# A hybrid encoder layer: the delta half of the output projection by pairs of chunks in seven block products, k and q loaded for two scan steps at once, both directions' decays in one load

## The chip, the cores and the metric

The kernel runs on one core of a Trainium2 chip. Its engines work side by side, each through its own instructions in order: TensorE (PE) multiplies matrices into PSUM, and its weight loads stand in rows of their own (PEld); VectorE (DVE), ScalarE (ACT) and GpSimd (POOL) work on elements; SyncE (SP) issues all DMA transfers of this kernel. The metric is the device time of one execution in microseconds. The kernel before took 1280.27 us (median of 3 runs, 1278.16 to 1280.57).

## The reference

A layer on 2048 positions of width 1024: a normalised input is projected once; one group of heads runs a gated delta rule in both directions, another runs windowed attention; both results are concatenated, projected, and added to the input.

```python
h = rms_norm(x, norm_w[l])
proj = h @ w_in[l]
dn = gated_deltanet_bidir(dn_q, dn_k, dn_v, dn_beta, dn_decay, ...)   # forward + flipped backward
dn = rms_norm(dn, dn_out_norm_w[l]).reshape(b, s, DN_WIDTH) * silu(dn_z)
sw = windowed_gqa_with_sinks(sw_q, sw_k, sw_v, ...) * silu(sw_z)
mix = concatenate([dn, sw], axis=-1)
x = x + mix @ w_out[l]
```

In the delta rule each of 4 heads carries a 128 x 128 state through the sequence, chunk by chunk:

```python
v_new = u_i - w_i @ state
o = (q_i * exp(g_i)) @ state + a_i @ v_new
state = state * exp(g_last) + k_dec.T @ v_new
```

All is in float32. The big projections split each operand into a high part rounded to fp32r and a low rest, and add three products (high-high, low-high, high-low).

## The kernel before, in words

The sequence is cut into 16 chunks of 128. The first part (phase_a) projects, convolves, runs the attention, and leaves in DRAM: k and q of each head (kq_d), v (v_d), the gates (zdn, zsw_d) and the attention's output (mix_sw). delta_setup computes decays: gr_d holds the cumulated decay rows of each direction, and for head 0 the finished decay matrices go to DRAM as dec.

The second part (phase_b) goes through the 4 heads. For each head, pre_front loads k and q by four chunks (kq), v (vt) and the decays (gm, shown as dc in the profile), transposes, and forms the chunks' matrices (ma); heads 1 to 3 load a decay row broadcast over 128 partitions (line 664), add a mask on POOL (L665) and take the exponential on ACT. solve and invert invert the chunk matrices (tiles iv, b, g; products pi). scan then runs both directions side by side through 16 steps. In one step of a direction, with its line: pk (L812) is k times the state, r (L814, DVE), py (L821), yk and y (L826, L828, ACT), po (L823, L830, L839), the new state S (L833, DVE), and the sum of the output oacc (L846 to L850). From the second step on, each step loads its chunk's k and q (kqc, L810), 128 KB, into one of four buffers per direction.

After step 12, and again after the last, post normalises two groups of four chunks: eight squares with their sums (jko, L864, ACT), a power on POOL (sso, L868), scaling (L875, ACT), transposition (tro, L878), times the gate (zt, L881, DVE), and a store to mix_dn (L882). The second half of the output projection, for the attention's heads (sw_units, products pcs, L599 to L601, 32 units of 12 matmuls), fills PE between the scans of the heads; its sums go to DRAM as part.

After the last head's inversion the pools of that work are closed (L913), and the first four blocks of w_out are loaded and split (load_wo, tiles wos, woh, wol). out_dn then makes one chunk of the output, in the order of ORD, that is 7, 8, 6, 9 and so on from the middle outwards, as the two directions of the scan finish them: the mixed features (mxd) are loaded and split (mhd on ACT, mld on DVE), each half of 512 columns takes 4 x 3 matmuls (pcd, L561 to L563) into a PSUM bank, part is loaded (xrd) and added (L564), and the result is stored. Line numbers of the changed kernel differ: there scan's matmuls stand at 786, 795, 797, 804 and 813, pcs at 570 to 572, the output's at 959 to 961.

What order an engine works in is set at the end: set_order collects all instructions with their dependencies, gives each a cost in ns (such as `return max(112, 0.441 * m + 4)` for an fp32r matmul of m columns, and a flat 500 for issuing a DMA), plans forward and backward twelve times, and fixes the best order found on each of the five engines. The order in the code matters only through dependencies; a change at one place can move rows anywhere. In these dependencies two accesses of a tensor count as overlapping without regard to its first dimension, and in mix_dn that is the head.

Of the kernel before, what the change touches and what calls it, by code (L numbers as in the profile page):

```python
# [7 lines left out]
F32 = mybir.dt.float32  # L8
# [7 lines left out]
P = 128  # L16
# [8 lines left out]
NDEC = 1  # L25
SCRATCH = 1024
# [404 lines left out]
def delta_setup(tc, t, ident, bd, gp, ap, bp, pj, q_pool):  # L431
# [64 lines left out]
    gr_d = q_pool.tile([2, 64, P], F32, tag="gr_d", name="gr_d")  # L496
    for d in range(2):
        gt = pj.tile([P, 512], F32, tag="pj", name=f"gt{d}")[:64, :P]
        T.transpose(gt, gc[:, d], ident)
        gs = s1[:64, (5 + d) * P : (6 + d) * P]  # L500
        V.tensor_copy(gs, gt)
        dma(gr_d[d], gs)
    dec_d = {}
    for h in range(NDEC):
        for d in range(2):
            dec_d[h, d] = q_pool.tile([4, P, 512], F32, tag=f"dec{h}_{d}", name=f"dec{h}_{d}")
        for c4 in range(4):
            s4 = slice(4 * c4, 4 * c4 + 4)
            for d in range(2):
                gm = ap.tile([P, 4, P], F32, tag="gm", name=f"gm{h}_{c4}_{d}", bufs=2)  # L510
                src = gr_d[d].rearrange("(c h) i -> c h i", h=4)[s4, h]
                dma(gm, src.partition_broadcast(P))
# [3 lines left out]
                dma(dec_d[h, d][c4], gm.rearrange("p c i -> p (c i)"))  # L516
# [3 lines left out]
def phase_b(ctx, wide, late, tc, t, ident, consts, hp, mix_dn, mix_sw, kq_d, v_d, zdn_d, zsw_d, dp, out):  # L520
# [15 lines left out]

    def load_wo(pool, k0, name, tg=""):
        wh = pool.tile([P, 4, D], F32R, tag="woh" + tg, name=f"woh{name}", bufs=1)
        wl = pool.tile([P, 4, D], F32R, tag="wol" + tg, name=f"wol{name}", bufs=1)
        for k in range(4):  # L540
            for j in range(2):
                ns = slice(j * 512, (j + 1) * 512)
                sw = pool.tile([P, 512], F32, tag="ws", name=f"wos{name}_{k}_{j}")
                dma(sw, t["wout"][:, k0 + k, ns])
                A.activation(wh[:, k, ns], sw, AF.Copy)
                V.tensor_tensor(wl[:, k, ns], sw, wh[:, k, ns].bitcast(F32), ALU.subtract)
        return wh, wl

    def out_half(pool, bank, w, mx, src, dst, name, nb):
        wh, wl = w  # L550
        mh = pool.tile([P, 4, P], F32R, tag="mh", name=f"mh{name}", bufs=nb)
        ml = pool.tile([P, 4, P], F32R, tag="ml", name=f"ml{name}", bufs=nb)
        A.activation(mh, mx, AF.Copy)
        V.tensor_tensor(ml, mx, mh.bitcast(F32), ALU.subtract)
        for j in range(2):
            ns = slice(j * 512, (j + 1) * 512)
            xr = pool.tile([P, 512], F32, tag="ws", name=f"xr{name}_{j}")
            dma(xr, src[:, ns])
            ps = bank(j, f"pc{name}_{j}")
            for k in range(4):  # L560
                T.matmul(ps, mh[:, k], wh[:, k, ns], start=(k == 0), stop=False)  # L561
                T.matmul(ps, ml[:, k], wh[:, k, ns], start=False, stop=False)  # L562
                T.matmul(ps, mh[:, k], wl[:, k, ns], start=False, stop=(k == 3))  # L563
            V.tensor_tensor(xr, xr, ps, ALU.add)  # L564
            dma(dst[:, ns], xr)
# [51 lines left out]
    q1 = pool("q1", stack=pre_stack)  # L617
# [19 lines left out]
    def pre_front(h):  # L637
# [12 lines left out]
        for n, c4 in enumerate(FRONT):  # L650
# [6 lines left out]
            gms = []  # L657
            for d in range(2):
                gm = q1.tile([P, 4, P], F32, tag="gm", name=f"dc{h}_{c4}_{d}", bufs=4)
                if h < NDEC:  # L660
                    dma(gm.rearrange("p c i -> p (c i)"), dec_d[h, d][c4])
                else:
                    src = gr_d[d].rearrange("(c h) i -> c h i", h=4)[s4, h]
                    dma(gm, src.partition_broadcast(P))
                    G.tensor_tensor(gm, gm, dmask[:, d : d + 1].to_broadcast([P, 4, P]), ALU.add)  # L665
                gms.append(gm)
# [131 lines left out]
    def scan(h, H):  # L798
        ks, vs, ck, ma = (H[k] for k in ("ks", "vs", "ck", "ma"))
        oacc = H["oacc"] = {}  # L800
        st = {}
# [109 lines left out]
    for k in range(32):  # L911
        fill(1, bank(k % 2))
# [396 lines left out]
```

## Time and profile before

| | |
|---|---|
| median of 3 runs | 1280.27 us (1278.16 to 1280.57) |
| profiled execution | 1274.25 us, of it span 1272.5 us |
| granted clock of PE, mean | 0.992 |
| PE busy | 1219.4 us (96%) |
| DVE, ACT, POOL busy | 889.5, 703.2, 507.4 us |
| DMA packets | 225510, 205.34 MB |

In rows of single instructions or groups, the first number is the start or the total in us, then follow engine, line, operation, output <- inputs, shape, and after the bar the busy time, the mean ns of one, and the idle time of that engine just before, with what ended it. A row of a window gives its length, then for each engine busy us and instructions in brackets, then the granted clock of PE (1.00 is full), the share of the 16 DMA engines and GB/s. A row of loads gives count, size of one, and the median us from issue to landing. An fp32 matmul is recorded as two passes. Matmuls are pipelined: one of 512 columns is shown with some 390 ns, while the next one starts earlier.

### The profile page before, as it was taken

How to read it: one execution, taken by the hardware profiler on the slowest of the kernel's cores; microseconds unless marked ns; L12 is line 12 of the kernel's file. 1: busy time of each engine (PE TensorE's matmuls, PEld its weight loads, DVE VectorE, ACT ScalarE, POOL GpSimd, SP SyncE). 2: the span in 40 equal slices, each digit the busy share in tenths (PEclk: the TensorE clock that was granted, in tenths of full speed). 3: DMA queues.
4: the chain of work that ended last, by engine and by line, in shares of the span. 5: the costliest groups of instructions: out<-in, count | busy, mean ns of one | idle time of the engine just before them, and what ended most of it. 6: DMA issues, size and time to landing. Idle time of an engine off the chain costs nothing.

```text
span 1272.5 us, 22253 instructions
## 1 busy us (share of the span) xinstructions
PE 1219.4 (96%) x7066; PEld 1044.4 (82%) x7066; DVE 889.5 (70%) x2154; ACT 703.2 (55%) x2105; POOL 507.4 (40%) x893
## 2 busy tenths in 40 slices
PE   6999999999999999999999998998799899999998
PEld 6998877788889998787788787887688789798876
DVE  4422387999975589999986573788488879557333
ACT  6321254776644677776654425858557955566210
POOL 1330044666613398665221306613672651641000
PEclk9999999999999999999999998999899999999999
DMA  8442254322544434522137826967965974746675
GB/s 269 145 132 76 95 180 128 97 97 81 180 132 144 130 96 116 158 87 67 58 117 244 224 96 189 276 189 207 270 169 154 269 191 138 217 145 214 227 242 205
DMA packets 225510, 205.34 MB, mean 161 GB/s; under 512 B 48497, under 2 KB 175089, under 8 KB 225393
## 3 DMA queue, kind: packets, MB, share of 16 engines
q1 hardware_dynamic: 225392, 203.92, 52.7%
q8 instruction: 56, 0.92, 0.3%
q14 instruction: 62, 0.50, 0.1%
HBM read 138.79 MB, written 65.08 MB: 160 GB/s over the span
## 4 chain that ended last, share of the span: by engine, by line
PE 67%; DVE 12%; DMA 9%; ACT 7%; issue 3%; POOL 1%; SPq 0%; DVEq 0%; ACTq 0%; POOLq 0%
PE pf_c L191 4%; PE pf_c L192 4%; PE pf_c L193 4%; PE pf_z L191 4%; PE pf_z L192 4%; PE pf_z L193 4%; PE pi L772 4%; DVE acc L242 3%; PE pt L363 3%; PE pq_q L202 2%; PE pq_q L204 2%; PE pq_q L203 2%; PE pcd L561 2%; PE pcd L563 2%; PE pcd L562 2%
## 5 line engine op out<-in xcount | busy, mean ns | idle before, releaser
L191 PE MATMUL pf_c<-xhi,wh_c 128*128 128x512 f32 x384 | 151.0, 404 | 0.7 <-DVE acc L242 0.4
L192 PE MATMUL pf_c<-xlo,wh_c 128*128 128x512 f32 x384 | 150.6, 401 | 0.0
L193 PE MATMUL pf_c<-xhi,wl_c 128*128 128x512 f32 x384 | 149.1, 401 | 0.0
L242 DVE SCALAR_TENSOR_TENSOR acc<-pf_c,cw,acc 128x512 f32<-128x512 f32 (+1 forms) x192 | 140.3, 743 | 11.3 <-ACT acc L238 9.2
L358 POOL TENSOR_SCALAR pr<-pr,st 128x384 f32<-128x384 f32 (+1 forms) x128 | 80.1, 648 | 71.3 <-DVE st L356 60.0
L191 PE MATMUL pf_z<-xhi,wh_z 128*128 128x512 f32 x256 | 86.6, 401 | 0.5 <-DVE zo L215 0.5
L349 ACT ACTIVATE pr<-pr,st 128x384 f32<-128x384 f32 (+1 forms) x128 | 76.1, 596 | 19.6 <-DVE st L345 19.1
L192 PE MATMUL pf_z<-xlo,wh_z 128*128 128x512 f32 x256 | 86.2, 399 | 0.0
L191 PEld LDWEIGHTS pf_c<-xhi,wh_c 128*128 128x128 f32 x384 | 72.1, 188 | 15.3 <-DVE acc L242 1.7
L193 PE MATMUL pf_z<-xhi,wl_z 128*128 128x512 f32 x256 | 84.7, 397 | 0.0
L192 PEld LDWEIGHTS pf_c<-xlo,wh_c 128*128 128x128 f32 x384 | 72.3, 188 | 13.0
L193 PEld LDWEIGHTS pf_c<-xhi,wl_c 128*128 128x128 f32 x384 | 71.8, 188 | 13.0
L345 DVE CUSTOM_DVE_ANT_0 pr<-s,mask,sink 128x384 f32<-128x384 f32 (+1 forms) x128 | 72.5, 593 | 12.4 <-PE s L344 8.3
L367 ACT ACTIVATE ph<-pt 128x512 fp32r<-128x512 f32 x92 | 53.0, 596 | 40.9 <-PE pt L363 39.1
L826 ACT ACTIVATE yk<-py,ck 128x128 f32<-128x128 f32 x120 | 43.9, 366 | 49.5 <-PE py L821 48.4
L363 PE MATMUL pt<-ident,pr 128*128 128x128 f32 x368 | 67.2, 274 | 1.9 <-DVE q L327 1.1
L368 DVE TENSOR_TENSOR pl<-pt,ph 128x512 fp32r<-128x512 f32 x92 | 61.6, 681 | 5.1 <-ACT ph L367 5.0
L703 DVE SCALAR_TENSOR_TENSOR ma<-gh,bp,dc 128x256 f32<-128x256 f32 x128 | 54.9, 476 | 10.4 <-PE gh L694 8.7
L363 PEld LDWEIGHTS pt<-ident,pr 128*128 128x128 f32 x368 | 46.5, 140 | 17.7 <-DVE pl L368 3.0
L202 PE MATMUL pq_q<-wh_q,xhi 128*128 128x256 f32 x256 | 60.3, 285 | 0.6 <-ACT sgkv L261 0.3
L599 PE MATMUL pcs<-wohs,mhs 128*128 128x512 f32 x128 | 57.7, 451 | 2.9 <-ACT mhs L593 2.3
L814 DVE SCALAR_TENSOR_TENSOR r<-pk,negc,vs 128x128 f32<-128x128 f32 x120 | 41.5, 346 | 27.1 <-PE pk L812 26.6
(251 smaller groups left out, 3709.8 us busy)
## 6 DMA issues: line engine op xcount, KB each, us to landing
kqc<-kq_d SPq DMA_DIRECT2D x120, 128.0 KB, 3.0
ws_c<-wt SPq DMA_DIRECT2D x48, 256.0 KB, 3.3
xr<-x SPq DMA_DIRECT2D x16, 512.0 KB, 6.3
ws_z<-wt SPq DMA_DIRECT2D x32, 256.0 KB, 3.9
kq<-kq_d SPq DMA_DIRECT2D x16, 512.0 KB, 5.3
m_d<-ma SPq DMA_DIRECT2D x32, 256.0 KB, 5.4
mxs<-mix_sw SPq DMA_DIRECT2D x32, 256.0 KB, 3.8
xrs<-x SPq DMA_DIRECT2D x32, 256.0 KB, 3.6
```

Of the source, the lines that this page charges most:

```text
L191: T.matmul(ps, hi[:, k, cs], xhi[b][:, k], start=(k == 0), stop=False)
L192: T.matmul(ps, hi[:, k, cs], xlo[b][:, k], start=False, stop=False)
L193: T.matmul(ps, lo[:, k, cs], xhi[b][:, k], start=False, stop=(k == KC - 1))
L202: T.matmul(ps[:, :n], xh, hi[:, k, :n], start=(k == 0), stop=False)
L242: V.scalar_tensor_tensor(av, ps[:, lo:], cw[:, i, k : k + 1], av, ALU.mult, ALU.add)
L345: V.tensor_tensor_reduce(pr[j][:, :n], ps[:, :n], mask[:, lo * P : hi * P], 1.0, sink[:, hh : hh + 1], ALU.add, ALU.min, accum_out=nm[:, j ...
L349: A.activation(pr[j][:, :n], pr[j][:, :n], AF.Exp, bias=nm[:, j : j + 1], scale=-1.0, accum_out=den[:, j : j + 1])
L358: G.tensor_scalar(pr[j][:, :n], pr[j][:, :n], den[:, j : j + 1], 1.0, ALU.mult, ALU.mult)
L363: T.transpose(pt[:, j], pr[j][:, (kb - lo) * P : (kb - lo + 1) * P], ident)
L368: V.tensor_tensor(pl, ptf, ph.bitcast(F32), ALU.subtract)
L599: T.matmul(ps, mh[:, k], wh[:, k], start=(k == 0), stop=False)
L703: V.scalar_tensor_tensor(ma[d, c4][:, c], gh[:, k], bp[:, d, cc : cc + 1], gms[d][:, c : c + 1].to_broadcast([P, 2, P]), ALU.mult, ALU.mult,)
```

## The change

Three things change.

The delta half of the output takes two chunks at once. With the features of a chunk cut in two halves (a11, a12 for one chunk, a21, a22 for the other) and w_out cut into four blocks (two feature halves, two column halves), the 2 x 2 block product is made of seven block products instead of eight, after a scheme of Strassen's kind: sums of the four feature blocks are made on POOL, and differences of the weight blocks too. Weights are laid into tiles that the heads have left (ma, ks, kq, gm, vt), so q1 stays open; they wait for these tiles, and not for the closing of the pools. One PSUM bank (p1) collects four products one after the other, and is read after each or copied (u2).

k and q are loaded for two steps in one transfer of 256 KB, into two buffers per direction in place of four. The decays of both directions lie side by side in DRAM, so one load brings both; the four chunks' rows of a head are contiguous there.

```diff
-    gr_d = q_pool.tile([2, 64, P], F32, tag="gr_d", name="gr_d")
+    gr_d = q_pool.tile([4, 2, NCH, P], F32, tag="gr_d", name="gr_d")
...
-        dma(gr_d[d], gs)
+        dma(gr_d[:, d].rearrange("h c i -> c h i"), gs)
...
-            gms = []
+            gms = q1.tile([P, 2, 4, P], F32, tag="gm", name=f"dc{h}_{c4}", bufs=2)
+            if h < NDEC:
+                dma(gms.rearrange("p d c i -> p d (c i)"), dec_d[h][c4])
+            else:
+                dma(gms.rearrange("p d c i -> p d (c i)"), gr_d[h][:, s4].rearrange("d c i -> d (c i)").partition_broadcast(P))
...
                 if i:
-                    kqc = rp.tile([P, 2, P], F32, tag=f"kqc{d}", name=f"kqc{nm}", bufs=4)
-                    dma(kqc, kq_d[h][:, :, sc])
+                    if i % 2:
+                        two[d] = rp.tile([P, 2, 2 * P], F32, tag=f"kqc{d}", name=f"kqc{nm}", bufs=2)
+                        n = min(2, NCH - i) * P
+                        c0 = c * P - (n - P) * d
+                        dma(two[d][:, :, :n], kq_d[h][:, :, c0 : c0 + n])
+                        low[d] = c0
+                    kqc = two[d][:, :, c * P - low[d] : (c + 1) * P - low[d]]
...
+            for p in (0, 4, 2, 6, 5, 1, 3):
+                if p == 4:
+                    G.tensor_tensor(b11, b12, b11, ALU.subtract)
+                elif p == 6:
+                    G.tensor_tensor(b12, b22, b12, ALU.subtract)
+                elif p == 5:
+                    G.tensor_tensor(b22, b22, b11, ALU.subtract)
+                elif p == 3:
+                    G.tensor_tensor(b21, b21, b22, ALU.subtract)
+                a = (b11, b21, b22, b21, b11, b22, b12)[p]
+                A.activation(wh[p][k], a, AF.Copy)
+                V.tensor_tensor(wl[p][k], a, wh[p][k].bitcast(F32), ALU.subtract)
...
+    def out_pair(c, e):
...
+                mx[x, k] = op.tile([P, 2, P], F32, tag="mx", name=f"mxd{x}_{k}", bufs=MXB)
+                dma(mx[x, k], mix_dn[2 * k : 2 * k + 2, :, x * P : (x + 1) * P].rearrange("f p s -> p f s"))
...
+        G.tensor_tensor(f[6], a11, a21, ALU.subtract)
+        G.tensor_tensor(f[4], a21, a22, ALU.add)
+        G.tensor_tensor(f[5], f[4], a11, ALU.subtract)
+        G.tensor_tensor(f[2], a12, f[5], ALU.subtract)
+        for hi, lo, x in (
+            (xh[0], xl[0], a11), (xh[1], xl[1], a12), (xh[3], xl[3], a22),
+            (bh[:, 3:6], bl[:, 3:6], S4[:, 0:3]), (xh[2], xl[2], f[2]),
+        ):
+            A.activation(hi, x, AF.Copy)
+            V.tensor_tensor(lo, x, hi.bitcast(F32), ALU.subtract)
+
+        def prod(ps, p, first):
+            for k in range(2):
+                on = dict(skip_group_check=not first)
+                T.matmul(ps, xh[p][:, k], wh[p][k], start=first and k == 0, stop=False, **on)
+                T.matmul(ps, xl[p][:, k], wh[p][k], start=False, stop=False, **on)
+                T.matmul(ps, xh[p][:, k], wl[p][k], start=False, stop=k == 1, **on)
...
+        o11 = row(c, 0)
+        prod(p1, 0, True)
+        V.tensor_tensor(o11, o11, p1, ALU.add)
+        prod(p2, 1, True)
+        V.tensor_tensor(o11, o11, p2, ALU.add)
+        put(c, 0, o11)
+        prod(p5, 4, True)
+        o22 = row(e, 1)
+        V.tensor_tensor(o22, o22, p5, ALU.add)
+        prod(p1, 5, False)
+        u2 = op.tile([P, 512], F32, tag="u2", name=f"u{nm}", bufs=U2B)
+        A.activation(u2, p1, AF.Copy)
+        prod(p5, 2, False)
+        o12 = row(c, 1)
+        V.tensor_tensor(o12, o12, p5, ALU.add)
+        G.tensor_tensor(o12, o12, u2, ALU.add)
+        put(c, 1, o12)
+        prod(p1, 6, False)
+        V.tensor_tensor(o22, o22, p1, ALU.add)
+        put(e, 1, o22)
+        prod(p1, 3, False)
+        o21 = row(e, 0)
+        V.tensor_tensor(o21, o21, p1, ALU.add)
+        put(e, 0, o21)
...
-    for c in ORD:
-        out_dn(c)
+    for c, e in zip(ORD[::2], ORD[1::2]):
+        out_pair(c, e)
```

row loads part for a chunk and a half of the columns (tile xrd), put stores the sum. The tiles of a pair: mh0d and ml0d hold the parts of a11, mhd and mld those of the other six operands, smd the four sums; wod the weights; pcd_0, pcd_1, pcd_2 are p1, p2, p5.

The order that set_order finds is another one on all engines from about the first third of the program on. Three places are shown. TensorE in the kernel before, where the first output matmul (pcd) meets the end of the last scan (py, pk, po are scan steps of head 3, with direction and step in the name):

```order
L601 MATMUL pcs_1_13944<-wols_13179,mhs_1_13938 128x512
L839 MATMUL po_1_13_14589<-y_1_13_14594,ma_3_13035 128x128
L812 MATMUL pk_1_14_14624<-S_1_13_14597,kqc_1_14_14622 128x128
L821 MATMUL py_0_14_14608<-r_0_14_14606,ma_3_13035 128x128
L823 MATMUL po_0_14_14609<-S_0_13_14577,kqc_0_14_14602 128x128
L830 MATMUL po_0_14_14609<-yk_0_14_14612,ks_3_13117 128x128
L821 MATMUL py_1_14_14628<-r_1_14_14626,ma_3_13035 128x128
L812 MATMUL pk_0_15_14644<-S_0_14_14617,kqc_0_15_14642 128x128
L823 MATMUL po_1_14_14629<-S_1_13_14597,kqc_1_14_14622 128x128
L839 MATMUL po_0_14_14609<-y_0_14_14614,ma_3_13035 128x128
L830 MATMUL po_1_14_14629<-yk_1_14_14632,ks_0_13041 128x128
L561 MATMUL pcd_0_14726<-wohd,mhd_14720 128x512
```

Output matmuls begin after step 14, and step 15 of both directions (8 matmuls) follows among them. TensorE in the changed kernel at the same place:

```order
L795 MATMUL py_0_15_14532<-r_0_15_14530,ma_3_12920 128x128
L786 MATMUL pk_1_15_14543<-S_1_14_14521,kqc_1_15_14541 128x128
L813 MATMUL po_1_14_14513<-y_1_14_14518,ma_3_12920 128x128
L797 MATMUL po_0_15_14533<-S_0_14_14503,kqc_0_15_14526 128x128
L813 MATMUL po_0_15_14533<-y_0_15_14536,ma_3_12920 128x128
L795 MATMUL py_1_15_14547<-r_1_15_14545,ma_3_12920 128x128
L797 MATMUL po_1_15_14548<-S_1_14_14521,kqc_1_15_14541 128x128
L813 MATMUL po_1_15_14548<-y_1_15_14551,ma_3_12920 128x128
L959 MATMUL pcd_0_14629<-wod_13842,mh0d_14610 128x512
```

There the last scan is through before the first output matmul, and the last matmul of the other half (pcs) stands 26 rows ahead of it, where it stood 11 rows ahead before. From the first transposition after step 12 (tro) on, 12 pcs rows followed before, and 2 follow now.

ScalarE in the kernel before, where the copies of the first chunks (mhd, from the second chunk on) meet the squares of the last normalisation (jko, three digits telling post, group and chunk):

```order
L553 ACTIVATE mhd_14760<-mxd_14758 128x512
L553 ACTIVATE mhd_14800<-mxd_14798 128x512
L553 ACTIVATE mhd_14840<-mxd_14838 128x512
L553 ACTIVATE mhd_14880<-mxd_14878 128x512
L553 ACTIVATE mhd_14920<-mxd_14918 128x512
L828 ACTIVATE y_1_15_14667<-py_1_15_14663 128x128
L864 ACTIVATE jko_0_0_0_14673,sso_0_14672<-oacc_0_14019 128x128
L864 ACTIVATE jko_0_0_1_14675,sso_0_14672<-oacc_0_14019 128x128
```

Six chunks are split ahead of the squares. ScalarE in the changed kernel, from the first copy of the first pair on:

```order
L953 ACTIVATE mh0d_14610<-mxd_0_14602 128x256
L838 ACTIVATE jko_0_0_0_14557,sso_0_14556<-oacc_0_13931 128x128
L838 ACTIVATE jko_0_0_1_14559,sso_0_14556<-oacc_0_13931 128x128
L838 ACTIVATE jko_0_0_2_14561,sso_0_14556<-oacc_0_13931 128x128
L838 ACTIVATE jko_0_0_3_14563,sso_0_14556<-oacc_0_13931 128x128
L838 ACTIVATE jko_0_1_0_14565,sso_0_14556<-oacc_3_13944 128x128
L838 ACTIVATE jko_0_1_1_14567,sso_0_14556<-oacc_3_13944 128x128
L838 ACTIVATE jko_0_1_2_14569,sso_0_14556<-oacc_3_13944 128x128
L838 ACTIVATE jko_0_1_3_14571,sso_0_14556<-oacc_3_13944 128x128
L953 ACTIVATE mhd_14612<-mxd_1_14606 128x256
L953 ACTIVATE mh0d_14703<-mxd_0_14695 128x256
```

One operand of the first pair (a11) is copied ahead of the squares, and all others behind them.

SyncE in the changed kernel where the first scan's k and q are loaded:

```order
L782 DMA kqc_0_1_8968<-kq_d_87 128x2x256
L782 DMA kqc_1_1_8988<-kq_d_87 128x2x256
L782 DMA kqc_0_3_9044<-kq_d_87 128x2x256
L221 DMA zdn_98<-zo_1_0_8428 128x512
L221 DMA zdn_97<-zo_1_1_8485 128x512
L221 DMA zdn_98<-zo_1_1_8485 128x512
L727 DMA xc_0_2_8789<-x_d_7751 128x4x32
L782 DMA kqc_1_3_9064<-kq_d_87 128x2x256
```

Four loads bring steps 1 to 4 of both directions, where eight of half the size stood before.

More of the change, by code (lines that the diff above doesn't have):

```diff
@@ L535, in phase_b @@
     part_d = [dp.tile([P, D], F32, tag=f"part{c}", name=f"part{c}") for c in range(NCH)]
[L537 to L565, printed above, removed]
     def sw_units(pool):
@@ L912, in phase_b @@
         fill(1, bank(k % 2))
[L913 to L923 removed]
+    pair = [P, 2, 512]
```

81 lines of the change are left out of this document (56 added, 25 removed).

## The prediction

> **What bounds the kernel now.** I read the page's busy shares and chain first, then the chain and the stages of the last 110 us, then the places where TensorE (PE) waits.
>
> ```profile
> PE 1219.4 (96%) x7066; PEld 1044.4 (82%) x7066; DVE 889.5 (70%) x2154; ACT 703.2 (55%) x2105; POOL 507.4 (40%) x893
> ...
> PE 67%; DVE 12%; DMA 9%; ACT 7%; issue 3%; POOL 1%; SPq 0%; DVEq 0%; ACTq 0%; POOLq 0%
> ...
> core 0: us, PE busy (x) PEld busy (x) DVE busy (x) ACT busy (x) POOL busy (x), PEclk, DMA share, GB/s
> 1100.00:1150.00 50.00, 48.02 (x360) 44.25 (x359) 25.42 (x76) 31.12 (x102) 24.81 (x62) 1.00 0.54 157
> 1168.40:1175.50 7.10, 6.28 (x39) 4.83 (x39) 7.10 (x19) 4.18 (x11) 0.00 (x0) 1.00 0.78 244
> 1175.50:1212.00 36.50, 36.17 (x171) 29.88 (x171) 15.43 (x33) 10.82 (x35) 1.64 (x1) 1.00 0.68 228
> 1212.00:1269.00 57.00, 55.74 (x241) 44.38 (x239) 19.12 (x32) 5.06 (x8) 0.00 (x0) 1.00 0.67 226
> ```
>
> PE is busy 96% of the span and holds 67% of the chain. The last three rows are the stage that the change rewrites: PE 55.74 of 57.00 us, VectorE (DVE) a third, POOL nothing. Here removed matmuls are removed time, unless something new makes PE wait. The chain shows how the stage is entered and paced:
>
> ```profile
> 1161.71 1.66 POOL sso L868
> ...
> 1170.10 4.87 DMA mix_dn<-zt
> 1174.98 4.78 DMA mxd<-mix_dn
> ...
> 1191.34 0.91 PE pcd L561 x4
> 1192.25 0.91 PE pcd L562 x4
> ...
> 1266.82 2.73 DVE xrd L564 x4
> ```
>
> Four output matmuls take 0.91 us, 0.227 each. And two idle stretches of PE show what a pause costs:
>
> ```profile
> 790.38 1.09 PE L674 MATMUL tr<-ident,kq 128*128 128x128 f32 x4 [3.86 <-DMA kq<-kq_d]
> ...
> 790.40:795.00 4.60, 4.60 (x22) 4.60 (x23) 2.38 (x6) 2.15 (x11) 0.31 (x2) 0.50 0.93 241
> ...
> 900.71 1.76 PE L694 MATMUL gh<-kq 128*128 128x256 f32 x4 [2.38 <-DVE ma L703]
> ...
> 902.50:905.00 2.50, 2.05 (x7) 1.52 (x8) 2.32 (x5) 2.50 (x9) 1.20 (x1) 0.50 0.85 268
> 905.00:907.50 2.50, 2.50 (x8) 1.92 (x7) 0.69 (x3) 1.10 (x4) 0.65 (x3) 0.50 0.88 178
> ```
>
> After 3.86 us and also after 2.38 us of idleness the granted clock is 0.50 for some 5 us, which loses about 2.3 us more.
>
> **The change, part by part.**
>
> *Seven products for eight.* Per pair of chunks 2 x 2 x 4 x 3 = 48 matmuls become 7 x 2 x 3 = 42; over 8 pairs 384 become 336. 48 x 0.227 = 10.9 us less PE work: **-10.9**.
>
> *Entering the stage.* The first output matmul needs the last scan's first normalisation (power on POOL, scaling on ScalarE (ACT), transposition, store, reload). Before, PE fills that time with the other half's matmuls (pcs) and starts output work inside the scan. In the changed order (first pair of listings under the change) the whole scan stands ahead of the first output matmul, and two pcs rows are left behind the first transposition where twelve stood.
>
> ```profile
> 1163.85 1.21 PE L878 MATMUL tro<-ident,oacc 128*128 128x128 f32 x4
> ...
> 1168.21 0.39 PE L823 MATMUL po<-S,kqc 128*128 128x128 f32 x2
> 1168.43 0.39 PE L830 MATMUL po<-yk,ks 128*128 128x128 f32 x2
> ...
> 1175.55 0.71 PE L561 MATMUL pcd<-wohd,mhd 128*128 128x512 f32 x2
> ```
>
> From the power's end (1163.4) to 1175.55 are 12.2 us. In them stand 8 transpositions (0.15 each), 12 pcs (0.227) and 21 scan rows (two passes, 0.22 by the second and third row): 8.5 us of work, 3.7 idle. After, the same chain (scaling, one transposed group more, store 4.87, reload 4.78 or less) gives about 12.5 us with 8 transpositions, 2 pcs and 25 scan rows: 7.2 us, 5.3 idle: **+1.6**; bounds 0 (a faster reload) and +5 (no fill at all).
>
> *The first pair.* On ACT (the listing of ScalarE under the change) the eight squares of the last normalisation now stand between the copy for the first product and that for the second.
>
> ```profile
> L864 ACT ACTIVATE jko<-oacc 128x128 f32<-128x128 f32 x16 | 4.7, 297 | 3.0 <-DVE oacc L850 3.0
> L864 ACT ACTIVATION_READ_ACCUMULATOR jko<-oacc 128x1 f32 x16 | 3.0, 188 | 0.0
> L553 ACT ACTIVATE mhd<-mxd 128x512 fp32r<-128x512 f32 x16 | 10.1, 633 | 62.7 <-PE pcd L563 60.1 <-DMA mxd<-mix_dn 2.6
> L828 ACT ACTIVATE y<-py 128x128 f32<-128x128 f32 x32 | 8.6, 270 | 0.0
> PE pcd L561 <- DVE mld L554: 1.1, 4, 0.3
> PE pcd L561 <- ACT mhd L553: 0.3, 1, 0.3
> ```
>
> Squares 8 x (0.297 + 0.188) = 3.9 us; a copy of 256 lies between 0.27 and 0.63, I take 0.4; one of 768 is about 0.9. PE has six matmuls (1.4 us) and then waits for 3.9 + 0.4, less what has run: 2.9 us; two matmuls later it waits 1.3 us for the 768-wide copy. 4.2 against the 1.4 us that the old stage waited: **+2.8**; bounds 0 (squares done before the reload lands) and +4.5 (POOL's sums late too). A pause of 2.9 us lies between 2.38 and 3.86, so I charge a half clock: **+2.3**, bounds 0 and +3.5.
>
> [...]
>
> *Steady state of the pairs.* A pair is 42 x 0.227 = 9.5 us of PE.
>
> ```profile
> L564 DVE TENSOR_TENSOR xrd<-xrd,pcd 128x512 f32<-128x512 f32 x32 | 20.6, 683 | 54.0 <-PE pcd L563 54.0
> L554 DVE TENSOR_TENSOR mld<-mxd,mhd 128x512 fp32r<-128x512 f32 x16 | 10.9, 684 | 2.0 <-ACT mhd L553 2.0
> L590 POOL TENSOR_TENSOR mxs<-mxs,zcs 128x512 f32<-128x512 f32 x6 | 7.6, 1274 | 22.7 <-DMA zcs<-zsw_d 22.6
> L545 ACT ACTIVATE wohd<-wosd 128x512 fp32r<-128x512 f32 x8 | 4.8, 634 | 2.5 <-DMA wosd<-wout 2.5
> ```
>
> DVE has six adds (4.1 us) and 1,792 columns of subtractions (2.4); POOL four sums of 256 (0.6 to 1.27 each) and one add, at most 6.4; ACT 1,792 columns of copies and one of 512, about 3. All fit in 9.5, and two PSUM sets let the next pair run while one is read: 0. Without that cover, each read of p1 (0.68 and two handoffs) would stop PE some 1 us. At the very end two adds follow each other instead of one: **+0.5** (0 to 0.7). Traffic stays: mxd becomes 32 loads of half the size.
>
> *The weights.* Eight loads, 14 copies (0.634), 14 subtractions (0.68) and 8 POOL differences (1.27) move into the last scan, past its k/q loads on SP. There DVE and POOL are half idle, ACT a third (row 1100 to 1150): 0. If POOL were full, three differences ahead of the last inversion's copies would delay it by 3.8 us.
>
> *Loads.* 120 k/q loads become 64 of up to 256 KB; 32 decay loads become 16, in longer pieces.
>
> ```profile
> kqc<-kq_d SPq DMA_DIRECT2D x120, 128.0 KB, 3.0
> ql<-q_d SPq DMA_DIRECT2D x16, 256.0 KB, 3.0
> kq<-kq_d SPq DMA_DIRECT2D x16, 512.0 KB, 5.3
> dc<-gr_d SPq DMA_DIRECT2D x24, 256.0 KB, 6.1
> 1110.04 0.39 PE L821 MATMUL py<-r,ma 128*128 128x128 f32 x2
> 1112.87 0.43 PE L821 MATMUL py<-r,ma 128*128 128x128 f32 x2
> 786.00:790.40 4.40, 0.54 (x6) 0.38 (x4) 1.18 (x2) 3.21 (x10) 3.95 (x13) 0.78 1.05 309
> ```
>
> A 256 KB load should land in 3.0 to 5.3 us. A k/q buffer now comes free after two steps, so a reload has two steps to land, 5.7 us at the fastest pace (1112.87 - 1110.04 = 2.83 a step), where it had three: just enough. In return the DMA engines, full while PE starved at 786 to 790 (share 1.05), have less to do: **-1.0**, between 0 and the whole hole, 3.86 + 2.3 = 6.2.
>
> Sum: -10.9 + 1.6 + 2.8 + 2.3 + 0.5 - 1.0 = **-4.7 us**. The profiled execution took 1274.25 us (span 1272.5), so 1269.6; it lies 6 us below the median of the runs, 1280.27, from which I predict **1275.6**.
>
> **The rivals.**
>
> *New holes at a change of heads* (other side). The order of everything from the first third on is redrawn, and the stretch 750 to 1000 already has two holes. For it: decay loads of both directions land together, so POOL's mask waits for twice as much (6.1 us for half). Against: fewer packets. A hole costs 6.2 us; one more than now leaves -4.7 + 6.2 = +1.5, two give +7.7, 1288. It decides from 7.3 us on.
>
> *k and q come late.* If SP is held 1.2 us longer than the slack in the last scan, six reload points cost 7.2 us: +2.5, 1282.8. Against it: over all four scans steps average far above 2.83 us.
>
> *It eats itself.* Entry and first pair cost 4 us more (bounds above): -0.7, 1279.6, no change.
>
> *No half clock, or a hole gone.* The first pair's pause stays short of what halves the clock, or the DMA relief closes the hole at 786: -7.0 to -10.9, 1273.3 to 1269.4. For it: a pause of 2.9 us is nearer to 2.38 than to 3.86, and other work may end it early; against it, 2.38 was enough once.
>
> **How the numbers follow.** Forecast 0.42, the better case 0.15, no change 0.18, holes 0.19, late k/q 0.06. 0.2% is 2.6 us, about what a measurement tells from nothing. Faster 0.57, same 0.18, slower 0.25. The forecast's own range is 1271.5 to 1278.5; to hold 8 in 10 the range goes from 1267 to 1288.
>
> **What would show it.** Output matmuls 336, still 0.227 apart between pairs; a PE wait of about 3 us on an ACT copy behind the squares, with a granted clock of 0.50 after it; no output matmul before the last scan step; k/q loads without a PE wait; the holes at 786 and 900 no wider. Wrong if pairs pace at more than 10 us (DVE, POOL or PSUM), if PE waits for k and q, or if the loss lies ahead of 1100 us.

## The result and the profile after

The changed kernel takes 1277.66 us (median of 17 runs, 1273.33 to 1283.19) against 1279.34 us before (17 runs, 1276.57 to 1286.84): ratio 0.9983, 95% interval 0.9971 to 0.9995. By the ratio that is 2.2 us less (0.6 to 3.7), just inside the 0.2% that the prediction set as the bound of a change. The forecast was 1275.6. The small number hides two large ones: the pairs alone take 8.0 us off, and the new loads put 5 us or more back on. The prediction had them at -3.7 and -1.0.

The page of the changed kernel, busy shares, traffic and chain:

```profile
PE 1212.8 (95%) x7018; PEld 1036.4 (81%) x7018; DVE 915.8 (72%) x2200; ACT 716.4 (56%) x2143; POOL 559.7 (44%) x941
...
DMA packets 197476, 205.33 MB, mean 161 GB/s; under 512 B 47600, under 2 KB 143472, under 8 KB 197360
...
q1 hardware_dynamic: 197360, 203.92, 52.0%
...
PE 63%; DVE 10%; DMA 9%; ACT 8%; POOL 5%; issue 4%; SPq 1%; ACTq 0%; POOLq 0%; DVEq 0%
```

The page's traffic lines of the kernel before:

```profile
DMA packets 225510, 205.34 MB, mean 161 GB/s; under 512 B 48497, under 2 KB 175089, under 8 KB 225393
...
q1 hardware_dynamic: 225392, 203.92, 52.7%
```

PE is 6.6 us less busy, yet the profiled execution is 3.1 us longer than the one shown of before (span 1275.6 against 1272.5): PE waits more than it did. The chain has passed from PE to POOL and ScalarE in part. And of the relief for the DMA engines little is there: 12% fewer packets, but their time falls only from 52.7 to 52.0% of the span.

The stage that was rewritten, from the end of the normalisation's power on POOL to the last output matmul, in three windows (entry, first pair or so, the rest). Columns are the stretch, its length, for PE, PEld, DVE, ACT and POOL busy time and count, then the granted clock, DMA share and GB/s. The windows of the kernel before:

```profile
1163.36:1175.55 12.19, 11.28 (x67) 8.41 (x66) 10.62 (x27) 9.16 (x26) 1.24 (x1) 1.00 0.69 219
1175.55:1200.00 24.45, 24.12 (x114) 19.76 (x113) 10.37 (x22) 4.31 (x8) 0.00 (x0) 1.00 0.65 223
1200.00:1268.82 68.82, 67.74 (x299) 54.44 (x297) 23.96 (x42) 11.57 (x36) 1.64 (x1) 1.00 0.68 228
sum 105.46, PE 103.14 PEld 82.62 DVE 44.95 ACT 25.04 POOL 2.88; mean PE 34.38 PEld 27.54 DVE 14.98 ACT 8.35 POOL 0.96
```

The same windows of the changed kernel:

```profile
1178.49:1189.42 10.93, 9.82 (x63) 7.61 (x61) 7.79 (x24) 4.80 (x17) 0.33 (x1) 1.00 0.61 178
1189.42:1200.00 10.58, 9.06 (x35) 6.34 (x34) 6.04 (x13) 8.82 (x34) 7.92 (x9) 0.84 0.90 298
1200.00:1271.96 71.96, 71.54 (x313) 57.60 (x311) 49.66 (x81) 16.93 (x37) 29.61 (x32) 1.00 0.72 237
sum 93.47, PE 90.42 PEld 71.55 DVE 63.49 ACT 30.56 POOL 37.86; mean PE 30.14 PEld 23.85 DVE 21.16 ACT 10.19 POOL 12.62
```

The stage is 12.0 us shorter. Some 2.3 us of that are ten pcs matmuls (0.227 each) that now run ahead of it, and some rows of the scan moved likewise. PE's idle time in it is 3.05 us (93.47 - 90.42) where it was 2.32. In the steady part PE idles 0.42 of 71.96 us: DVE (49.66) and POOL (29.61) are well covered. What the stage won is lost before it: it starts 15.1 us later (1178.49 against 1163.36), of which those pcs are 2.3 and some is chance, since the profiled execution of before was 5 us under the median of its runs.

### The profile page after: what moved, and what is told of

It reads as the page before. It is cut to its first block, busy times and chain, and to the rows that moved or that the text cites. A ratio compares the mean times of both kernels' runs of the same rounds, so it can differ in the third digit from the quotient of the medians.

```text
span 1275.6 us, 22153 instructions
## 1 busy us (share of the span) xinstructions
PE 1212.8 (95%) x7018; PEld 1036.4 (81%) x7018; DVE 915.8 (72%) x2200; ACT 716.4 (56%) x2143; POOL 559.7 (44%) x941
## 3 DMA queue, kind: packets, MB, share of 16 engines
q1 hardware_dynamic: 197360, 203.92, 52.0%
## 4 chain that ended last, share of the span: by engine, by line
PE 63%; DVE 10%; DMA 9%; ACT 8%; POOL 5%; issue 4%; SPq 1%; ACTq 0%; POOLq 0%; DVEq 0%
PE pf_c L194 5%; PE pf_c L195 5%; PE pf_c L196 5%; PE pf_z L194 4%; PE pf_z L195 4%; PE pf_z L196 4%; DVE acc L245 3%; PE pt L366 3%; PE pi L742 2%; PE pq_q L205 2%; PE pq_q L207 2%; PE pq_q L206 2%; PE pcd L959 2%; PE pcd L961 2%; PE pcd L960 2%
## 5 line engine op out<-in xcount | busy, mean ns | idle before, releaser
L654 POOL TENSOR_TENSOR nk<-ssk,pw 128x4 f32<-128x4 f32 x16 | 16.6, 1038 | 104.3 <-DVE ssk L653 104.2
```

## The experiments

Three readings stood against each other: (A) the new loads cost the scans time; (B) the order of all engines, which the planner draws anew whenever anything changes, costs it; (C) the one pair of profiles misleads and nothing is lost.

### One part alone, and the order drawn anew

e1_loads is the kernel before with the new loads only (k and q for two steps, decays of both directions in one load). e2_pairs is the changed kernel with the old loads put back; since the decay buffers are four again, the tiles of one weight product change with them:

```diff
-    w = [spare(q1, [P, 2, 512], "gm", f"wod5_{x}", 2) for x in range(2)]
-    wh.append([w[0][:, k] for k in range(2)])
-    wl.append([w[1][:, k] for k in range(2)])
+    w = [spare(q1, flat, "gm", f"wod5_{x}", 4) for x in range(4)]
+    wh.append(w[:2])
+    wl.append(w[2:])
```

> The kernel before with only the loads changed: k and q for two steps at once, decays of both directions in one load; the output stage stays as it was. The forecast puts this at -1.0 us (ratio 0.9992). Theory A (the changed loads cost the scans what the profiles show as a loss of some 11 us ahead of 1181 us): +7 to +11 us, ratio 1.0055 to 1.0085. Theory B (the loss comes from the order, which is drawn anew whatever is changed, and not from the loads): anything from -5 to +5 us, and the place of the loss is another than in the changed kernel. Theory C (the one profiled pair misleads, nothing is lost in the middle): within 1 us of 0.

> The changed kernel with the loads of before: k and q step by step, decays by direction; the output by pairs of chunks in seven products stays (one weight product's tiles are four single ones, since the decay buffers are four). The forecast puts this at -10.9 + 1.6 + 2.8 + 2.3 + 0.5 = -3.7 us (ratio 0.997). Theory A (the loads cost the middle 7 to 11 us): the gain at the end stands alone, -8 to -10 us, ratio 0.992 to 0.994. Theory B (the order costs it): -10 to 0 us, with holes at other places than the changed kernel's. Theory C: -2 to -4 us.

c_before_draw and c_after_draw change one number that only the planner sees:

```diff
-            return 500
+            return 500 + 10 * o[0].tensor.name.startswith("kqc")
```

> The kernel before, with one number of the planner changed: issuing a k/q load of the scans counts 510 ns in place of 500. The program is the same, the order of all engines is drawn anew from about half way on. Theory B: the time moves by 2 to 6 us, up or down, and holes of PE appear or close at the changes of heads. Theories A and C: within 1.5 us of the kernel before (0.999 to 1.001).

> The changed kernel, with the same number of the planner changed (510 ns for 500): the order differs only from the last third of the third scan on. Theory B: the time moves by 2 to 6 us against the changed kernel, up or down. Theories A and C: within 1.5 us of the changed kernel, ratio to the kernel before 0.997 to 0.9995.

| run | median us | ratio to the kernel before, 95% interval |
|---|---|---|
| changed kernel | 1277.66 | 0.9983 (0.9971 to 0.9995) |
| e1_loads | 1284.32 | 1.0029 (1.0014 to 1.0043) |
| e2_pairs | 1272.44 | 0.9937 (0.9918 to 0.9955) |
| c_before_draw | 1275.49 | 0.9954 (0.9936 to 0.9971) |
| c_after_draw | 1277.79 | 0.9972 (0.9956 to 0.9989) |

The loads alone make the kernel slower by 3.7 us, the pairs alone make it faster by 8.0: reading C falls. The 3.7 us also lie below the 7 to 11 that reading A gave for the loads. And B isn't out: merely drawing the order of the old program anew is worth 5.9 us, between the two parts in size; with the changed kernel it is worth nothing that can be told (1.4 us, inside the intervals). So a part can only be priced with the order held.

### The same order, other loads

The next kernels hold the order of the four computing engines to that of another run, instruction for instruction, by a chain of constraints in the planner; only the DMA queue (SP) is planned for the loads at hand. The computing instructions are the same in both, so only the loads, their buffers and the order of the queue differ:

```diff
+    for e, pos in held.items():
+        mine = [k for k in range(n) if insts[k][1] == e]
+        for a, b in zip(pos, pos[1:]):
+            nxt[mine[a]].append((mine[b], None))
+            prv[mine[b]].append((mine[a], None))
```

> The changed kernel, its pairs and its loads, but with the order of the four computing engines held instruction for instruction to that which the planner drew for the pairs with the loads of before (run e2_pairs, 0.9937); only the DMA queue is planned for the new loads. Theory A (the loads themselves cost time: two steps of k and q come late, the decays land late): 0.996 to 0.999, as the changed kernel, with PE waits on the loads or on what they feed. Theory B (the order costs it): 0.992 to 0.995, as e2_pairs.

> The kernel before with only the loads changed, as e1_loads (1.0029), but with the order of the four computing engines held instruction for instruction to that of the kernel before. Theory A: still 1.002 to 1.004. Theory B: 0.998 to 1.001; the forecast of -1.0 us lies in that.

> The pairs with the loads of before, as e2_pairs (0.9937), but with the order of the four computing engines held to that of the changed kernel. Theory A: 0.992 to 0.995, since the loads are those of before. Theory B: 0.997 to 0.9995, as the changed kernel, although none of its loads is left.

| order drawn for | old loads | new loads | the loads cost |
|---|---|---|---|
| kernel before (no pairs) | 1.0000 | h_loads_before 1.0052 (1.0029 to 1.0075) | 6.7 us |
| e2_pairs | e2_pairs 0.9937 (0.9918 to 0.9955) | h_after_e2 0.9993 (0.9972 to 1.0014) | 7.2 us |
| changed kernel | h_pairs_after 0.9944 (0.9924 to 0.9964) | changed kernel 0.9983 (0.9971 to 0.9995) | 5.0 us |

Across a row only the loads change, with their buffers and queue, and each time 5 to 7 us go; down the two rows with pairs only the order changes, and nothing happens that can be told. The loss belongs to the loads, in any of three orders: theory A. It isn't that loads were put into an order made for others: the third order was drawn for the new loads, and the old ones still do better in it. The 1.0052 of h_loads_before is more than theory A expected of it.

Since the orders are the same, the start of each PE instruction can be subtracted between two traces, and a step in the difference is a place where time is lost. From before to h_loads_before the largest step behind the first 60 us is 3.3 us, at 724.87 (of before). The timeline of the kernel before there, PE and the two engines ahead of it (start, us, engine, line, output and input, and in brackets the idle time before it and who ended it):

```profile
724.87 0.51 PE L191 MATMUL pf_z<-xhi,wh_z 128*128 128x512 f32 x1 [0.49 <-DVE zo L215]
...
721.87 2.55 POOL L665 TENSOR_TENSOR dc<-dc,dmask 128x512 f32<-128x512 f32 x2 [3.02 <-DMA dc<-gr_d]
...
723.21 0.40 ACT L702 ACTIVATE dc<-dc,ngc 128x128 f32<-128x128 f32 x1 [3.06 <-POOL dc L665]
723.51 1.06 ACT L214 ACTIVATE zo<-pf_z 128x512 f32<-128x512 f32 x2
```

The same rows in h_loads_before:

```profile
731.98 0.79 PE L194 MATMUL pf_z<-xhi,wh_z 128*128 128x512 f32 x1 [3.83 <-DVE zo L218]
...
729.03 2.48 POOL L666 TENSOR_TENSOR dc<-dc,dmask 128x512 f32<-128x512 f32 x2 [4.81 <-issue]
...
730.33 0.40 ACT L702 ACTIVATE dc<-dc,ngc 128x128 f32<-128x128 f32 x1 [6.40 <-POOL dc L666]
730.63 1.06 ACT L217 ACTIVATE zo<-pf_z 128x512 f32<-128x512 f32 x2
```

The view of the decay tile dc in the kernel before, 715 to 735 us (issues with their length in ns, first and last start, and the time to landing):

```profile
L664 SPq DMA_DIRECT2D dc<-gr_d x2: 637/650/664, 715.8 to 716.5; - x2
...
DMA to landing us min/median/max: 6.0/6.2/6.4
```

And in h_loads_before:

```profile
L662 SPq DMA_DIRECT2D dc<-gr_d x1: 458/458/458, 721.3 to 721.3; - x1
...
DMA to landing us min/median/max: 7.6/7.6/7.6
```

The decays of head 1 were issued at 715.8 and 716.5, two halves, each landing 6.0 to 6.4 us later. As one load they are issued at 721.3 and land after 7.6 us. PE runs 3.8 us later here already, so the load is 1.7 us late at its issue and 1.4 us in flight. Nothing of PE reads these decays. But POOL's masks wait for them, ScalarE's first exponential waits for the mask, the activation that reads pf_z (zo) stands behind it on ScalarE, DVE's product zo stands behind that, and PE waits for the PSUM bank that this product frees: 3.83 us instead of 0.49. h_after_e2 has the same wait at 730.71 (3.79 against 0.65 us in e2_pairs).

The other common step is at 1016, and it isn't at a load that was changed. The timeline of h_pairs_after there, PE and ScalarE:

```profile
1012.91 0.66 PE L687 MATMUL trv<-ident,vt 128*128 128x128 f32 x4 [0.33 <-ACT jk L658]
...
1016.09 0.50 PE L575 MATMUL pcs<-wohs,mhs 128*128 128x512 f32 x1 [0.62 <-ACT vs L691]
...
1014.09 0.63 ACT L552 ACTIVATE wohs<-woss 128x512 fp32r<-128x512 f32 x1 [0.94 <-DMA woss<-wout]
```

The same of the changed kernel, with the queue ahead of that weight load (SPq rows are issues):

```profile
1010.35 0.66 PE L681 MATMUL trv<-ident,vt 128*128 128x128 f32 x4 [0.34 <-ACT jk L652]
...
1015.74 0.80 PE L570 MATMUL pcs<-wohs,mhs 128*128 128x512 f32 x1 [2.85 <-ACT vs L685]
1016.34 0.63 PE L571 MATMUL pcs<-wohs,mls 128*128 128x512 f32 x1
1016.76 0.63 PE L572 MATMUL pcs<-wols,mhs 128*128 128x512 f32 x1
1017.19 0.63 PE L570 MATMUL pcs<-wohs,mhs 128*128 128x512 f32 x1
...
1013.74 0.63 ACT L547 ACTIVATE wohs<-woss 128x512 fp32r<-128x512 f32 x1 [3.15 <-DMA woss<-wout]
...
1002.34 1.35 SPq L782 DMA_DIRECT2D kqc<-kq_d  x2
1003.79 0.55 SPq L678 DMA_DIRECT2D m_d<-ma  x1
1004.57 0.38 SPq L632 DMA_DIRECT2D dc<-gr_d  x1
1006.03 0.52 SPq L782 DMA_DIRECT2D kqc<-kq_d  x1
1006.66 0.56 SPq L546 DMA_DIRECT2D woss<-wout  x1
```

The view of the tile woss at this place, in h_pairs_after:

```profile
DMA to landing us min/median/max: 4.8/4.8/4.8
```

And in the changed kernel:

```profile
DMA to landing us min/median/max: 7.1/7.1/7.1
```

From trv to pcs PE takes 5.39 us where it took 3.18: 2.2 us lost, and the matmuls behind it are 0.43 apart, at a granted clock of 0.50. ScalarE waits for woss, a load that nobody changed, and vs, for which PE waits, stands behind that copy. It took 7.1 us instead of 4.8, and ahead of it, in the one queue, now stand three k/q loads of 256 KB and a decay load of 512 KB, all issued within 4 us. That decay load alone takes 7.4 us to land; its two halves of 256 KB took 5.4 and 5.6 in h_pairs_after. Transfers land in the order of their issue here: of the 831 that SP issues in the changed kernel, none lands before an earlier one.

The changed kernel's own hole near 720 is of this second kind. At 721.25 PE waits 1.48 us for DVE's product ma; DVE stands behind ScalarE's copy of ws_z, and ScalarE waits for ws_z, again a load that nobody changed. It lands after 8.8 us, issued behind a merged decay load, where the one in h_pairs_after lands after 6.1.

### Which load, and by what

Three parts were taken apart, all with the order of the changed kernel, so that 0.9944 (neither load) and 0.9983 (both) are the ends. h_p_kqc loads the decays by direction again, h_p_dec loads k and q step by step again, and h_p_split keeps the decay tile for both directions but fills it with two transfers:

```diff
-            if h < NDEC:
-                dma(gms.rearrange("p d c i -> p d (c i)"), dec_d[h][c4])
+            for d in range(2):
+                if h < NDEC:
+                    dma(gms[:, d].rearrange("p c i -> p (c i)"), dec_d[h][c4][:, d])
```

(and so for the heads whose decays come from gr_d).

> The changed kernel with the decays loaded by direction again, into four buffers of 256 KB; k and q still for two steps at once; the order of the four computing engines held to that of the changed kernel. With neither load changed this order gave 0.9944 (h_pairs_after), with both 0.998. Theory D (the merged decays are late: 7.1 to 7.6 us to land where a half landed in 6.2, and both directions wait for both): 0.993 to 0.9955, the holes near 720 and 1015 us gone. Theory K (k and q for two steps are late or hold the queue up): 0.997 to 0.999.

> The changed kernel with k and q loaded step by step again; the decays of both directions still in one load; the order of the four computing engines held to that of the changed kernel. Theory D: 0.997 to 0.999, the loss stays. Theory K: 0.993 to 0.9955. If both loads cost about half each, both runs come out at 0.995 to 0.9975.

> The changed kernel, its decay tile for both directions and its two buffers kept, but each direction's half loaded by a transfer of its own of 256 KB; k and q for two steps; the order of the four computing engines held to that of the changed kernel. If theory D holds and the length of the one transfer is what costs: 0.993 to 0.9955. If theory D holds and the coarser buffer is what costs (no half can be loaded before both halves of the older tile are used): 0.997 to 0.999. Under theory K: 0.997 to 0.999 as well, but then h_p_dec has no loss.

h_p_split2 also fills the k/q tiles by two transfers of the old size, one in each step:

```diff
-                        dma(two[d][:, :, :n], kq_d[h][:, :, c0 : c0 + n])
...
+                    dma(kqc, kq_d[h][:, :, c * P : (c + 1) * P])
```

> The changed kernel with all its buffers (k and q in two tiles of two steps, decays in two tiles of both directions) but every tile filled by two transfers of the old sizes, each step's k and q and each direction's decays by its own; the order of the four computing engines held to that of the changed kernel. Theory L (the long transfers cost: they put 128 to 256 KB that are not needed yet ahead of the loads that something waits for, in a queue that serves in order): the loss goes, 0.993 to 0.9955. Theory G (the coarser buffers cost: no half can be loaded before the whole older tile has been used): the loss stays, 0.997 to 0.999. Half of each: 0.9955 to 0.997.

The table has the ratio, and how much later PE is than in h_pairs_after, instruction against instruction, stretch by stretch (us of h_pairs_after). Each row is one execution. The first 60 us are left out: two executions differ there by up to 5 us at the same instruction.

| run | ratio | 60 to 690 | 690 to 760 | 760 to 960 | 960 to 1060 | 1060 to 1200 | to the end |
|---|---|---|---|---|---|---|---|
| changed kernel | 0.9983 | -1.0 | +1.8 | +0.8 | +3.4 | +1.2 | 0.0 |
| h_p_kqc | 0.9951 (0.9930 to 0.9972) | -0.4 | -0.2 | +0.1 | +3.0 | -0.9 | +0.4 |
| h_p_dec | 0.9958 (0.9940 to 0.9976) | 0.0 | 0.0 | +1.6 | +1.6 | 0.0 | 0.0 |
| h_p_split | 0.9974 (0.9957 to 0.9992) | -0.1 | -0.1 | +0.2 | +3.2 | +2.5 | -0.3 |
| h_p_split2 | 0.9971 (0.9954 to 0.9988) | -2.2 | +0.3 | +4.0 | +2.7 | -1.5 | -0.6 |

Neither theory D (decays) nor K (k and q) gets the loss to itself. Each load alone costs 0.9 and 1.8 us, which the intervals don't separate from nothing or from half of the 5.0; by the medians both together (5.0) cost more than the sum of the two (2.7), which the intervals don't show. Of these five, only the changed kernel has the loss at 720; the one at 1016 comes with any of them. Smaller transfers into the same coarse tiles win 1 us or so back, not the 5 (0.9974 and 0.9971, where theory G said 0.997 to 0.999 and L 0.993 to 0.9955), though the intervals are wide. That speaks against the length of a transfer as such. It doesn't separate the coarser buffers from the early bytes, and the loss at 1016 shows why. Its weight load woss comes late in two ways. The table has its issue against the start of the transposition of kq that PE makes just before (tr, at 1010.59 in h_pairs_after), and its time to landing:

| run | woss issued, us from tr | issue to landing, us |
|---|---|---|
| h_pairs_after | 1.35 before | 4.8 |
| changed kernel | 1.36 before | 7.1 |
| h_p_split | 1.35 before | 7.2 |
| h_p_dec | 0.57 before | 5.6 |
| h_p_kqc | 0.06 after | 5.4 |
| h_p_split2 | 0.88 after | 5.2 |

In the changed kernel and in h_p_split it is issued in time and lands late. In the last three it lands almost as fast as with the old loads, but is issued 0.8 to 2.2 us later: just ahead of it in the queue now stands a k/q load (kqc) that waits for PE's transpositions, which none does there in the first three. The queue is planned anew in each of these runs, so its order is a possible cause beside the buffers and the bytes, and none of them holds it.

### The first pair

h_after_squares is the changed kernel in its own order on all engines and the queue, with the eight squares of the last normalisation moved on ScalarE behind the first pair's copies:

```diff
 mh0d7 <- mxd7_0
-jko3_0 <- oacc3 (x8)
 mhd7 <- mxd7_1
 mh0d6 <- mxd6_0
 mhd7 <- mxd8_1
 mhd7 <- smd7 (768 wide)
+jko3_0 <- oacc3 (x8)
```

> The changed kernel in its own order, held on all engines and on the DMA queue, except that on ScalarE the eight squares of the last normalisation stand behind the copies of the first pair instead of between its first and second. The prediction charged these squares 2.8 us of waiting and 2.3 us of half clock. If that was right: 4 to 5 us less than the changed kernel, ratio 0.9935 to 0.9955. If the trace of the changed kernel is right (PE waits 1.4 us for the subtraction behind the first copy, then runs some ten matmuls at 0.42 instead of 0.23 us): 1 to 3 us less, 0.9955 to 0.9975. If the squares are needed in time for the second normalisation group and its loads come late: no gain, 0.998 or above.

It came out at 0.9980 (0.9962 to 0.9998): no gain over 0.9983 that can be told. The timeline of the changed kernel at the first output matmuls, PE, DVE and ScalarE:

```profile
1189.42 0.50 PE L959 MATMUL pcd<-wod,mh0d 128*128 128x512 f32 x1
1191.31 0.50 PE L960 MATMUL pcd<-wod,ml0d 128*128 128x512 f32 x1 [1.40 <-DVE ml0d L954]
...
1190.30 0.96 DVE L954 TENSOR_TENSOR ml0d<-mxd,mh0d 128x256 fp32r<-128x256 f32 x1
...
1190.35 0.31 ACT L838 ACTIVATE jko<-oacc 128x128 f32<-128x128 f32 x1 [0.98 <-DVE oacc L824]
1190.57 0.19 ACT L838 ACTIVATION_READ_ACCUMULATOR jko<-oacc 128x1 f32 x1
1190.66 0.29 ACT L838 ACTIVATE jko<-oacc 128x128 f32<-128x128 f32 x1
...
1192.70 0.40 ACT L953 ACTIVATE mhd<-mxd 128x256 fp32r<-128x256 f32 x1
```

The pauses of PE at the same place in h_after_squares:

```profile
1187.51 0.51 PE L963 MATMUL pcd<-wod,ml0d 128*128 128x512 f32 x1 [1.04 <-DVE ml0d L957]
...
1191.85 0.54 PE L963 MATMUL pcd<-wod,mld 128*128 128x512 f32 x1 [1.62 <-DVE mld L957]
```

And the sum over the windows of the stage, from the power's end to the last output matmul, in h_pairs_after, which has the order of the changed kernel and no half clock there:

```profile
sum 93.09, PE 89.14 PEld 70.93 DVE 63.13 ACT 30.67 POOL 37.72; mean PE 29.71 PEld 23.64 DVE 21.04 ACT 10.22 POOL 12.57
```

A square with its read of the sum takes 0.31 us (1190.35 to 1190.66), so the eight end at 1192.7. PE's first pause isn't theirs: it waits for the subtraction ml0d, which DVE begins only at 1190.30, behind the scan's last additions, and which takes 0.96 us. With the squares out of the way that pause is 1.04 us, and one of 1.62 us, for the next subtraction, appears nine matmuls later; the half clock then begins there.

What the squares do cost can be seen in h_pairs_after, which has the order of the changed kernel and stays at full clock there. PE waits twice for copies that stand behind them, 1.0 us together:

```profile
1190.82 0.50 PE L961 MATMUL pcd<-wod,mhd 128*128 128x512 f32 x1 [0.48 <-ACT mhd L955]
...
1192.16 0.73 PE L961 MATMUL pcd<-wod,mhd 128*128 128x512 f32 x2 [0.54 <-ACT mhd L955]
```

## Why the prediction came near, and where it was wrong

The sum of -4.7 us was near the measured -2.2 because its two halves were off by 4 us and by 6 us or more, with opposite signs. That is luck.

- **Seven products for eight, -10.9**: right. The steady part of the stage has 71.54 of 71.96 us busy, and neither DVE, POOL nor PSUM paces the pairs.
- **Entry +1.6**: oversized. The windows give 0.91 us of idle PE in the old entry and 1.11 in the new one: +0.2. The working had 3.7 us of idleness before, from counts times durations (8.5 of 12.2 us); the window says 11.28 busy. That step failed: idleness was worked out as a remainder instead of read.
- **First pair +2.8**: oversized, and the wrong wait. The first pause, 1.40 us, is for DVE's subtraction and not for a copy behind the squares. PE idles 1.52 us in the 10.58 us that begin with the first output matmul, against 0.33 in the old stage's first 24.45: +1.2. A square was charged 0.485 us, activation and read of the sum one after the other; they overlap, 0.31. The waits for copies behind the squares come to 1.0 us in h_pairs_after.
- **Half clock +2.3**: it came, at 1191.7, for 3.41 us, but behind a pause of 1.40 us and not of 2.9. It adds 1.3 us of busy PE: the changed kernel's stage has 90.42 us, and h_pairs_after, the same instructions in the same order without it, 89.14. The stage is only 0.4 us longer (93.47 against 93.09), since PE at half clock doesn't meet the two waits for copies: its idle time in the stage is 3.05 us, where h_pairs_after has 3.95. The two stretches from which the 2.3 us were worked out last 6.83 us each in the trace of before.
- **Steady state and end, 0 and +0.5**: idle time of the last window fell by 0.7 us (1.08 to 0.42), and from the last output matmul to the end of the span are 3.6 us where 3.7 were: the second add at the end cost nothing that can be seen.

Of 7.2 us charged against the pairs about 2.0 came, so -8.9 by the trace; the run alone has -8.0 (-5.8 to -10.5), where the prediction had -3.7.

- **Loads: 0 and -1.0**: the step that failed most. They cost 5.0 to 7.2 us. "The DMA engines have less to do" failed on its size: 28,034 packets fewer, 0.7% of the span less time, and the hole at 786 has a wait of 3.9 us for kq as before. "Just in time" was right as far as it went, PE never waits for a k/q load of the scans (kqc) in the changed kernel. It was the wrong question: the k/q and decay loads don't come late for their own readers alone, they make others late that stand behind them in the queue (woss 7.1 us where it took 4.8), and the engines, each in its fixed order, hand that on to PE (2.85 us of waiting at 1015.74 in the changed kernel). The loss lies ahead of 1100 us, at 720 and 1016, which the prediction had named as a sign that it was wrong.

The rival of new holes at a change of heads had the right mechanism for the hole at 720 in h_loads_before and h_after_e2: decays of both directions land together and POOL's masks wait (4.81 us in h_loads_before, 3.02 before). In the changed kernel the hole there comes over the weights behind the decays. The rival got 0.19 and a price of 6.2 us a hole; the steps there were 1.7 to 3.3 us, and the better tail covered them. The rival that the reload of k and q starves PE is out. No change, 0.18, is what the ratio shows, but the rival that stood for it ("it eats itself") had the cause in the entry and the first pair, and these cost less than charged.

Three things stay open. The runs don't say which of the two loads costs more, nor what part of it is due to the coarse buffers, to the bytes fetched early and to the order of the queue. And why another drawing of the old program's order is 5.9 us faster isn't shown: the profile of before is one of its quickest executions (1274.25 us, below all 17 runs of the median), so its trace can't be set against that of c_before_draw. With it goes a doubt on the pairs: two orders of them agree (0.9937 and 0.9944) and the stage's own windows explain their 8 us, but against the lucky drawing of the old program they are only 2.2 us faster.

The version that beats both kernels is the pairs with the old loads: 0.9937 in its own order, 0.9944 in that of the changed kernel.

## What to carry to other kernels

Merging loads was not free in this kernel, whose one queue landed all its transfers in the order of their issue: it cost 5.0 to 7.2 us. A merged load put bytes that were not needed yet ahead of one that something waited for (woss, 7.1 us for 4.8), and its buffer comes free only when both halves are used, which can have held the queue: between 700 and 1180 us the longest wait of the queue at a k/q load was 8.2 us in the changed kernel and 3.8 in h_pairs_after. Look for who stands behind a load, not only for who reads it. Where a planner redraws everything, hold its order before pricing a part: a redraw by itself moved this kernel by 5.9 us. And read idle time from a window of the trace instead of working it out as what is left over.

## What the hardware showed that was not expected

The half clocks of one trace lie whole multiples of one length apart. In the traces of before and of the changed kernel each stretch at a granted clock of 0.50 between 60 us and the end of the output matmuls lasts 3.41 us or twice that, and the stretches of one trace begin whole multiples of 3.413 us apart: in the changed kernel at 792.34, 904.98, 1014.21 and 1191.70 (33, 32 and 52 steps), in the kernel before at 788.43, 901.07 and 924.97 (33 and 7). Each of these began behind a step with 0.66 to 1.92 us of busy PE. In windows of one step (3.41 us) each, the step with the first pair's pause and the one behind it. The changed kernel:

```profile
1188.32:1191.73 3.41, 1.92 (x10) 1.32 (x10) 2.50 (x8) 1.96 (x11) 2.15 (x3) 1.00 0.98 287
1191.73:1195.14 3.41, 3.29 (x9) 2.00 (x8) 1.58 (x5) 3.41 (x15) 2.29 (x4) 0.50 0.98 332
```

h_pairs_after:

```profile
1186.61:1190.02 3.41, 2.07 (x10) 1.47 (x10) 1.85 (x6) 2.43 (x16) 2.30 (x3) 1.00 1.00 304
1190.02:1193.44 3.42, 2.40 (x10) 1.44 (x9) 2.23 (x5) 3.08 (x12) 3.29 (x4) 1.00 0.88 295
```

h_after_squares:

```profile
1188.78:1192.20 3.42, 1.71 (x7) 0.86 (x6) 1.59 (x5) 3.41 (x20) 2.08 (x3) 1.00 0.99 341
1192.20:1195.61 3.41, 3.41 (x11) 2.66 (x10) 1.74 (x3) 2.27 (x8) 3.25 (x4) 0.50 0.52 176
```

1.92 and 1.71 us of busy PE in a step were followed by the half clock, 2.07 by the full one. In the traces of before and of the changed kernel, over the same stretch of time, all six steps at full clock with up to 1.49 us of busy PE (1.49 in that from 785.02, before) were followed by half clock, and none with more than 1.92. In between it went both ways: in the changed kernel 1.92 us (from 1188.29) was followed by it, 1.87 and 1.91 (from 911.81 and 1120.02) weren't. So a pause of 1.40 us was followed by a half clock, and one of 1.87 us (h_pairs_after at 917.22) wasn't, though the step that holds most of it (913.52 to 916.93) has 1.84 us of busy PE, less than the 1.92 above: in that range the busy time of one step doesn't settle it, and what does stays open.

Longer pieces made the transfers hardly cheaper: with 12% fewer packets the queue's packets took 52.0 instead of 52.7% of the span for the same 203.92 MB. The packets that became fewer are those of 512 B (88,320 before, 43,264 after), and in the trace of the changed kernel a packet of 512 B takes 28.0 ns on the mean and one of 1,024 B 53.7, 1.92 times as long for twice the bytes.
